# A squared-ReLU MLP by seven products: eight output pairs run their first two products ahead, with results kept in DRAM

## The chip, the cores and the metric

The kernel runs on one core of a Trainium2 chip. Its engines are TensorE (PE; weight loads are shown as PEld), VectorE (DVE), ScalarE (ACT), GpSimd (POOL) and SyncE (SP), whose queue issues nearly all DMA transfers. The metric is the device time of one execution in microseconds; lower is better.

## The reference, cut to what matters

One inference step of a decoder layer: attention and a state-space mixer side by side, then an MLP. The changed code is all in the MLP, over T = 1032 tokens (1024 of a prompt and 8 decoded ones):

```python
x = x + mixed @ w_out                       # (1032, 1024)
u = rms_norm(x, norm_mlp) @ w_up            # 1024 -> 4096
x = x + jnp.square(jax.nn.relu(u)) @ w_down # 4096 -> 1024
```

All values are float32.

## The kernel before, in words

Everything is kept transposed: features on the 128 partitions, tokens along the free axis. Each float32 operand is split (`split`, L131 and L132) into a high part, rounded by ACT to `fp32r`, and a low part, the rest, made by DVE; each product is then three matmuls (high x high, high x low, low x high) that add up in PSUM.

The MLP's first matrix product is computed in blocks. Tokens fall into two halves of HT = 516 columns (H0, H1), input features into two halves of 512 (four partition tiles each), output features into 16 pairs of tiles (2m, 2m+1). For each pair m, seven block products instead of eight make the four output blocks, after sums of weight blocks and of x blocks (a scheme of Strassen's kind). Each product is 4 feature tiles x 3 matmuls x 2 column halves of HC = 258, that is 24 matmuls. They are, in the order of the loop (L1493):

- A: `w1[0:4]` by the first x block (`b11`), copied by ACT to the tile `p1` (`first_product`), then `w1[4:8]` by the second (`b21`) on top of it (`second_product`); the result, after relu and square (`emit_u`, ACT), is stored to the DRAM tensor `u_d`. These two need only the first token half, which is normed and split into `bpr` early.
- five more products, of the weight sums w2, w3, w4 and the x blocks `xva[VT2]`, `VT3`, `VT1`, `VT4`, `V22`, which need the second token half. DVE adds `p1` and PSUM results (L1522, L1528, L1531, L1536, L1540), and six more stores to `u_d` follow.

In this text a pair that runs all seven in the loop is a whole pair, one that runs five a short pair, and the two products run ahead of the loop are an early pair.

Where the second half begins (L1458): the norm factors of that half must be made (`half_stats`, `half_bcast`), then for each of four q the blocks in `xrow` are normed (L1370) and combined (L1473 to L1478; L1477 and L1478 run on POOL), and 20 blocks are split into `xvt`. To give PE something to do meanwhile, the first FP = 4 pairs run as early pairs, with `p1` kept in SBUF (`p1s`).

Weights come from DRAM into `wraw` (two buffers of 512 KB). `wslot` hands out split buffers in a rotation of six: the first two are the `wh`/`wl` buffers of the pool `wp`, the next four are pairs of the pool `opl`, which has eight pairs and whose first eight hold `xrow` (four) and `bpr` (four). `w_first` takes its weights from `wslot`. A whole pair takes four slots, a short pair three.

Preparation of a pair (L1494 to L1510): two raw loads `ra` and `rw`, the additions s1 (L1501), s2, and two in place, and the splits of w2, w3, w4.

The second matrix product (L1569) runs over e, eighths of 512 features of u: load the squares from `u_d` (L1575) through a small tile, split them into four pairs of the pool `up` (6 buffers), which is opened after the pools of the first product are closed, then for each of eight output tiles n three column blocks (384, 384, 264) of 12 matmuls, added by DVE to accumulators `dacc` (L1591).

Within an engine, instructions run in a fixed order that the framework's scheduler has set when the program was built; it need not be the order of the source. A tile that takes over a buffer waits for the last reader of the tile before it.

Of the kernel before, what the change touches and what calls it, by code (L numbers as in the profile page):

```python
# [8 lines left out]
F32 = mybir.dt.float32  # L9
# [45 lines left out]
def hybrid_step(ctx: ExitStack, tc: tile.TileContext, I, O):  # L55
# [3 lines left out]
    def pool(name, bufs=1, **kw):  # L59
        return tc.tile_pool(name=name, bufs=bufs, reuse_waits="tile", **kw)  # L60
# [1312 lines left out]
    NM = 16  # L1373
    FP = 4
    p1s = {}
    slots = [0]
# [81 lines left out]

    xv = mst.enter_context(pool("xv", 1, side="right"))
    VT2, VT3, VT1, VT4, V22 = range(5)  # L1460
    xvt = [[tuple(xv.tile([P, HT], F32R, name=f"x{v}{q}{t}") for t in "hl") for q in range(4)] for v in range(5)]
    xva = [chunk_of(xvt[v], 0) for v in range(5)]
    wa = {0: w_first(0), 1: w_first(1)}
    A = first_product(0, wa[0])
    sv = half_stats(1)
# [3 lines left out]
    for q in range(4):  # L1469
        x11, x12, x21, x22 = xrow[q][:, H0], xrow[q][:, H1], xrow[q + 4][:, H0], xrow[q + 4][:, H1]  # L1470
        normed(q, H1, rb1)
        normed(q + 4, H1, rb1)
        V.tensor_tensor(x11, x12, x11, ALU.subtract)  # L1473
        t2 = mp.tile([P, HT], F32, tag="sa", name="t2")
        V.tensor_tensor(t2, x22, x11, ALU.subtract)
        split(*[t[:] for t in xvt[VT2][q]], t2)
        G.tensor_tensor(x12, x22, x12, ALU.subtract)  # L1477
        G.tensor_tensor(x21, x21, t2, ALU.subtract)  # L1478
        if q:
            if q > 1:  # L1480
                wa[q] = w_first(q)
            A = first_product(q, wa[q])
            second_product(q, wa[q], A)
    for q in range(4):
        split(*[t[:] for t in xvt[VT3][q]], xrow[q][:, H1])
    for q in range(4):
        split(*[t[:] for t in xvt[VT1][q]], xrow[q][:, H0])
    for q in range(4):
        split(*[t[:] for t in xvt[VT4][q]], xrow[q + 4][:, H0])
    for q in range(4):  # L1490
        split(*[t[:] for t in xvt[V22][q]], xrow[q + 4][:, H1])

    for m in range(NM):  # L1493
# [25 lines left out]
        for s in range(2):  # L1519
            prod(X[s], w2, 0, xva[VT2](s), True)  # L1520
            u2.append(mp.tile([P, HC], F32, tag="u2", name="u2"))
            V.tensor_tensor(u2[s], X[s], pc[s], ALU.add)  # L1522
        if m >= FP:
            second_product(m, w1, A)
        for s in range(2):
            prod(X[s], w2, 4, xva[VT3](s), False)
            u3.append(mp.tile([P, HC], F32, tag="u3", name="u3"))
            V.tensor_tensor(u3[s], X[s], pc[s], ALU.add)  # L1528
        for s in range(2):
            prod(Y[s], w3, 0, xva[VT1](s), True)  # L1530
            V.tensor_tensor(u3[s], u3[s], Y[s], ALU.add)  # L1531
            emit_u(2 * m + 1, HT + s * HC, u3[s])
        for s in range(2):
            prod(X[s], w3, 4, xva[VT4](s), False)
            c21 = mp.tile([P, HC], F32, tag="ca", name="c21")
            V.tensor_tensor(c21, X[s], pc[s], ALU.add)  # L1536
            emit_u(2 * m + 1, s * HC, c21)
        for s in range(2):
            prod(Y[s], w4, 0, xva[V22](s), False)
            V.tensor_tensor(u2[s], u2[s], Y[s], ALU.add)  # L1540
            emit_u(2 * m, HT + s * HC, u2[s])
# [27 lines left out]
    for e in range(NE):  # L1569
        ups = [pair(up) for _ in range(FE)]  # L1570
        for c0, cn in CH:
            cs = slice(c0, c0 + cn)
            for f in range(FE):
                r = yp.tile([P, 384], F32, tag="ld", name="ld", bufs=4)
                DQ.dma_start(r[:, :cn], u_d[e * FE + f, :, cs])  # L1575
                split(ups[f][0][:, cs], ups[f][1][:, cs], r[:, :cn])
        uh = lambda k: ups[k][0]
        ul = lambda k: ups[k][1]
        for n2 in range(4):
# [59 lines left out]
```

## Time and profile before

| | |
|---|---|
| runs | 2250.95, 2255.86, 2258.33 us; median 2255.86 |
| the profiled execution | 2256.27 us, span 2254.5 us |
| granted TensorE clock, mean | 0.981 of 2.4 GHz |
| PE busy | 2162.6 us, 96% |
| DVE, ACT, POOL busy | 1365.1, 1013.6, 348.0 us |
| DMA moved | 252.32 MB, mean 112 GB/s |

Times in the profile are microseconds from the start of the span. Matmuls are pipelined, so one shown as 0.28 us follows the one before after 0.12 us; for the length of a piece of work the starts are compared. A part "idle before" in brackets is the time that an engine waited, and what released it. Some matmul records can be missing.

### The profile page before, as it was taken

To read this page: it belongs to the slowest core of one execution; us is meant where nothing else is said; L and a number is where in the kernel's file an instruction comes from. 1 tells how busy PE (TensorE), PEld (TensorE's weight loads), DVE (VectorE), ACT (ScalarE), POOL (GpSimd) and SP (SyncE) were. 2 spreads that over 40 slices of the span, in tenths; PEclk is the share of its full clock that TensorE was granted. 3 is DMA by queue.
4 is the path that set the end of the run, shared out by engine and by line. 5 is a ranking of instruction groups with operands and counts; after the bars stand their busy time and mean duration, and the time that the engine had idled before them with its cause. 6 is when DMAs were issued, how large, how long until landed. Compare 5 with 4: busy or idle time off the path is not lost. (4 is left out here: it accounts for less than half of the span.)

```text
span 2254.5 us, 39182 instructions
## 1 busy us (share of the span) xinstructions
PE 2162.6 (96%) x14859; PEld 2057.8 (91%) x14859; DVE 1365.1 (61%) x2893; ACT 1013.6 (45%) x2044; POOL 348.0 (15%) x409
## 2 busy tenths in 40 slices
PE   6999999998999999999999999996999999999998
PEld 5988899897888898877999999995999998999998
DVE  6778787336846666677355867468655544554452
ACT  3255665235647656666343333345555542221122
POOL 3232232001213222223200013222000000000000
PEclk8999999999999999999999999998999999999999
DMA  4232233322324224123475766642333336332222
GB/s 134 80 109 67 82 90 96 89 61 67 95 67 125 54 82 117 48 81 106 132 229 178 239 186 187 176 146 83 105 109 109 111 98 186 98 110 86 81 93 85
DMA packets 348052, 252.32 MB, mean 112 GB/s; under 512 B 34473, under 2 KB 343929, under 8 KB 347823
## 3 DMA queue, kind: packets, MB, share of 16 engines
q1 hardware_dynamic: 346247, 248.54, 37.3%
q8 instruction: 117, 1.92, 0.4%
q10 hardware_dynamic: 1616, 1.28, 0.2%
q14 instruction: 72, 0.59, 0.1%
HBM read 176.04 MB, written 71.56 MB: 110 GB/s over the span
## 5 line engine op out<-in xcount | busy, mean ns | idle before, releaser
L148 PE MATMUL mm<-hT_h,wh 128*128 128x384 f32 (+1 forms) x1536 | 502.2, 327 | 0.4 <-ACT spill L231 0.4
L149 PE MATMUL mm<-hT_l,wh 128*128 128x384 f32 (+1 forms) x1536 | 493.1, 321 | 0.0
L150 PE MATMUL mm<-hT_h,wl 128*128 128x384 f32 (+1 forms) x1536 | 492.6, 321 | 0.0
L148 PEld LDWEIGHTS mm<-hT_h,wh 128*128 128x128 f32 x1536 | 290.8, 189 | 13.4 <-issue 12.2
L149 PEld LDWEIGHTS mm<-hT_l,wh 128*128 128x128 f32 x1536 | 290.6, 189 | 0.0
L150 PEld LDWEIGHTS mm<-hT_h,wl 128*128 128x128 f32 x1536 | 290.4, 189 | 0.0
L131 ACT ACTIVATE wh<-wraw 128x1024 fp32r<-128x1024 f32 (+1 forms) x158 | 159.9, 1013 | 276.1 <-PE dn L149 153.4
L148 PE MATMUL mm<-oh,wh 128*128 128x384 f32 (+2 forms) x832 | 256.8, 309 | 1.0 <-ACT pr L1289 1.0
L150 PE MATMUL mm<-oh,wl 128*128 128x384 f32 (+2 forms) x832 | 256.3, 308 | 1.4 <-DVE wl L132 1.4
L132 DVE TENSOR_TENSOR wl<-wraw,wh 128x1024 fp32r<-128x1024 f32 (+1 forms) x158 | 185.9, 1177 | 117.1 <-ACT wh L131 111.7
L149 PE MATMUL mm<-ol,wh 128*128 128x384 f32 (+2 forms) x832 | 256.4, 308 | 0.0
L148 PE MATMUL dn<-oh,wh 128*128 128x384 f32 (+1 forms) x768 | 246.4, 323 | 4.2 <-ACT oh L131 4.2
L149 PE MATMUL dn<-ol,wh 128*128 128x384 f32 (+1 forms) x768 | 248.5, 324 | 1.0 <-DVE ol L132 1.0
L150 PE MATMUL dn<-oh,wl 128*128 128x384 f32 (+1 forms) x768 | 246.8, 321 | 0.0
L1591 DVE TENSOR_TENSOR dacc<-dacc,dn 128x384 f32<-128x384 f32 x168 | 85.9, 511 | 151.7 <-PE dn L150 151.7
L148 PEld LDWEIGHTS mm<-oh,wh 128*128 128x128 f32 x832 | 156.6, 188 | 1.7 <-ACT pr L1289 1.5
L150 PEld LDWEIGHTS mm<-oh,wl 128*128 128x128 f32 x832 | 156.6, 188 | 1.6 <-DVE wl L132 1.6
L149 PEld LDWEIGHTS mm<-ol,wh 128*128 128x128 f32 x832 | 156.5, 188 | 0.0
L148 PEld LDWEIGHTS dn<-oh,wh 128*128 128x128 f32 x768 | 145.1, 190 | 5.1 <-ACT oh L131 4.9
L149 PEld LDWEIGHTS dn<-ol,wh 128*128 128x128 f32 x768 | 145.7, 190 | 3.6 <-DVE ol L132 3.4
L150 PEld LDWEIGHTS dn<-oh,wl 128*128 128x128 f32 x768 | 145.5, 189 | 0.0
L131 ACT ACTIVATE oh<-ld 128x384 fp32r<-128x384 f32 (+1 forms) x105 | 48.4, 487 | 122.3 <-PE dn L150 65.1
(952 smaller groups left out, 4573.6 us busy)
## 6 DMA issues: line engine op xcount, KB each, us to landing
wraw<-in_w_in SPq DMA_DIRECT2D x64, 512.0 KB
wraw<-in_w_up SPq DMA_DIRECT2D x36, 512.0 KB
u_d<-u SPq DMA_DIRECT2D x128, 129.0 KB
wraw<-in_w_down SPq DMA_DIRECT2D x32, 512.0 KB
ld<-u_d SPq DMA_DIRECT2D x64, 192.0 KB
xt<-in_x_prompt SPq DMA_DIRECT2D x16, 512.0 KB
s<-in_state_ssm SPq DMA_DIRECT2D x32, 256.0 KB
out_ssm_sample<-s SPq DMA_DIRECT2D x32, 256.0 KB
```

The lines of the kernel that those rows point to most:

```text
L131: first = S.activation(h, src, AF.Copy)
L132: second[:] = [V.tensor_tensor(l, src, h.bitcast(F32), ALU.subtract)]
L148: TE.matmul(ps, lhsT=a, rhs=h, start=k == 0, stop=False)
L149: TE.matmul(ps, lhsT=a, rhs=l, start=False, stop=False)
L150: TE.matmul(ps, lhsT=b, rhs=h, start=False, stop=k == kt - 1)
L1591: V.tensor_tensor(ac[:, cs], prev, ps[:, :cn], ALU.add)
```

## The change

FP goes from 4 to 8: eight early pairs. Their `p1` is stored to a new DRAM tensor `p1_d` and loaded again when the pair's short part runs. Early weights are taken from the two `wh`/`wl` buffers only, not from `wslot`, each traced one early pair ahead; the early pairs are spread over the norming loop and the splits that follow it. The two subtractions that ran on POOL run on DVE. The x blocks live in tiles of T columns (`x23`, `x14`) and `x22`, in a pool that stays open to the end, and these tiles then take the split squares of the second product: `load_ups(0)` is traced in the last pair, `load_ups(e + 1)` ahead of the products of eighth e. The pool `up` is gone, and the accumulators move to the left side of SBUF.

```diff
+    p1_d = dr.tile([8, P, T // 2], F32, name="p1_d")
-    FP = 4
-    p1s = {}
+    FP = 8
     def first_product(m, w):
         p1 = p1t("p1")
-        p1s[m] = p1
         A = [bank(s) for s in range(2)]
         for s in range(2):
             prod(A[s], w, 0, b11(s), True)
             S.activation(p1[:, s * HC:(s + 1) * HC], A[s], AF.Copy)
-        return A
+        if m < FP:
+            DQ.dma_start(p1_d[m], p1)
+        return A, p1
     def w_first(m):
         raw = raw_up(2 * m * P)
-        w = wslot()
+        w = tuple(wp.tile([P, KT, P], F32R, tag=t, name=t) for t in ("wh", "wl"))
         split(w[0], w[1], raw)
         return w
+    def xpair(i):
+        return tuple(xv.tile([P, T], F32R, tag=f"x{i}{t}", name=f"x{i}{t}") for t in "hl")
+    x23 = [xpair(q) for q in range(4)]
+    x14 = [xpair(4 + q) for q in range(4)]
+    def early(m):
+        second_product(m, wa[m], first_product(m, wa[m])[0])
     for q in range(4):
...
-        G.tensor_tensor(x12, x22, x12, ALU.subtract)
-        G.tensor_tensor(x21, x21, t2, ALU.subtract)
-        if q:
-            if q > 1:
-                wa[q] = w_first(q)
-            A = first_product(q, wa[q])
-            second_product(q, wa[q], A)
+        V.tensor_tensor(b12_, b22_, b12_, ALU.subtract)
+        V.tensor_tensor(b21_, b21_, t2, ALU.subtract)
+        early(q + 1)
+        wa[q + 2] = w_first(q + 2)
     for q in range(4):
-        split(*[t[:] for t in xvt[VT3][q]], xrow[q][:, H1])
+        split(x23[q][0][:, H1], x23[q][1][:, H1], xrow[q][:, H1])
+    early(5)
+    wa[6] = w_first(6)
...
+    early(6)
+    wa[7] = w_first(7)
...
+    early(7)
...
+    def load_ups(e, home, step):
+        ups[e] = [xpair(4 * (e % 2) + f) for f in range(4)]
+        for c0 in range(0, T, step):
+            cn = min(step, T - c0)
+            cs = slice(c0, c0 + cn)
+            for f in range(4):
+                r = home()
+                DQ.dma_start(r[:, :cn], u_d[e * 4 + f, :, cs])
+                split(ups[e][f][0][:, cs], ups[e][f][1][:, cs], r[:, :cn])
     for m in range(NM):
...
         if m >= FP:
-            A = first_product(m, w1)
-        p1 = p1s.pop(m)
+            A, p1 = first_product(m, w1)
+        else:
+            p1 = p1t("p1")
+            DQ.dma_start(p1, p1_d[m])
...
+        if m == NM - 1:
+            load_ups(0, lambda: p1t("ld"), HT)
...
-    up = ctx.enter_context(pool("up", 6, side="right"))
-    dap_ = ctx.enter_context(pool("dap", 1, side="right"))
+    dap_ = ctx.enter_context(pool("dap", 1))
...
     for e in range(NE):
-        ups = [pair(up) for _ in range(FE)]
...
+        if e + 1 < NE:
+            load_ups(e + 1, lambda: yp.tile([P, 384], F32, tag="ld", name="ld", bufs=4), 384)
```

In the last pair `load_ups(0)` stands between the products of `x23`'s second half and the three that remain.

## Rows read from the trace of the kernel before

**Rows 1.** The page, part 1: busy time, share of the span, instructions.

```profile
PE 2162.6 (96%) x14859; PEld 2057.8 (91%) x14859; DVE 1365.1 (61%) x2893; ACT 1013.6 (45%) x2044; POOL 348.0 (15%) x409
```

**Rows 2.** PE's waits, 1500 to 2254: waiting line and releaser, total, times, longest.

```profile
PE mm L1398 <- ACT oh L131: 21.0, 1, 21.0
PE dn L148 <- ACT oh L131: 4.2, 1, 4.2
PE dn L1398 <- DVE u L1522: 4.0, 1, 4.0
```

**Rows 3.** Timeline of PE: start, duration, engine, line, operation, out<-in, shape, idle before.

```profile
1523.09 0.28 PE L1400 MATMUL dn<-oh,wl 128*128 128x258 f32 x1
1544.40 0.58 PE L1398 MATMUL mm<-oh 128*128 128x258 f32 x1 [21.03 <-ACT oh L131]
...
1557.88 0.28 PE L1398 MATMUL mm<-x00h,oh 128*128 128x258 f32 x1
...
1572.31 0.28 PE L1398 MATMUL mm<-x00h,wh 128*128 128x258 f32 x1
...
1593.16 0.28 PE L1398 MATMUL mm<-x00h,oh 128*128 128x258 f32 x1
...
1622.81 0.28 PE L1398 MATMUL mm<-oh 128*128 128x258 f32 x1
...
1861.91 0.28 PE L1398 MATMUL mm<-x40h,oh 128*128 128x258 f32 x1
...
1869.14 0.69 PE L148 MATMUL dn<-oh,wh 128*128 128x384 f32 x1 [4.17 <-ACT oh L131]
...
1886.29 0.34 PE L148 MATMUL dn<-oh,wh 128*128 128x384 f32 x1
...
1908.98 0.34 PE L148 MATMUL dn<-oh,wh 128*128 128x384 f32 x1
```

**Rows 4.** Windows of 10 us: PE, PEld, DVE, ACT, POOL busy; granted clock, DMA share, GB/s.

```profile
1540.00:1550.00 10.00, 5.57 (x31) 5.27 (x32) 10.00 (x15) 3.52 (x5) 0.28 (x1) 0.59 0.23 62
1550.00:1560.00 10.00, 10.00 (x86) 10.00 (x85) 8.23 (x14) 6.39 (x15) 0.00 (x0) 1.00 0.34 94
...
1580.00:1590.00 10.00, 9.21 (x58) 9.21 (x59) 7.08 (x14) 4.88 (x11) 0.00 (x0) 0.72 0.24 68
...
1920.00:1930.00 10.00, 9.74 (x56) 8.75 (x56) 7.12 (x15) 4.72 (x10) 0.00 (x0) 1.00 0.63 187
1930.00:1940.00 10.00, 10.00 (x66) 10.00 (x65) 5.27 (x10) 2.00 (x3) 0.00 (x0) 1.00 0.42 131
```

**Rows 5.** Timeline of DVE, 1519 to 1547, columns as in rows 3.

```profile
1519.00 1.42 DVE L1370 SCALAR_TENSOR_TENSOR oh<-oh,prm,rb 128x516 f32<-128x516 f32 x2 [0.97 <-ACT rb L1367]
...
1522.22 1.79 DVE L1370 SCALAR_TENSOR_TENSOR ol<-ol,prm,rb 128x516 f32<-128x516 f32 x1
...
1539.07 1.76 DVE L132 TENSOR_TENSOR x11l<-ol,x11h 128x516 fp32r<-128x516 f32 x1
...
1544.39 1.21 DVE L132 TENSOR_TENSOR ol<-wraw,oh 128x1024 fp32r<-128x1024 f32 x1
1545.53 0.68 DVE L132 TENSOR_TENSOR x23l<-ol,x23h 128x516 fp32r<-128x516 f32 x1
1546.13 0.68 DVE L132 TENSOR_TENSOR x30l<-oh,x30h 128x516 fp32r<-128x516 f32 x1
```

**Rows 6.** Timeline of SP's queue: issues of DMA, columns as in rows 3.

```profile
1505.55 0.38 SPq L1389 DMA_DIRECT2D wraw<-in_w_up  x1
1506.66 3.20 SPq L1342 DMA_DIRECT2D x_d<-ol  x2
...
1572.66 0.38 SPq L1389 DMA_DIRECT2D wraw<-in_w_up  x1
```

**Rows 7.** Timeline of DVE, 1574 to 1581, columns as in rows 3.

```profile
1578.98 0.69 DVE L1501 TENSOR_TENSOR s<-wraw 128x512 f32<-128x512 f32 x1 [4.52 <-DMA wraw<-in_w_up]
...
1580.32 0.42 DVE L1522 TENSOR_TENSOR u<-dn,p 128x258 f32<-128x258 f32 x1
```

**Rows 8.** The chain of work that ended last, at the up product's end.

```profile
1865.34 3.15 DMA ld<-u_d
```

More of the change, by code (lines that the diff above doesn't have):

```diff
@@ L1456, in hybrid_step @@
     rst.close()
[L1459 to L1462, printed above, removed]
+    xv = ctx.enter_context(pool("xv", 1, side="right"))
+    def xpair(i):
+        return tuple(xv.tile([P, T], F32R, tag=f"x{i}{t}", name=f"x{i}{t}") for t in "hl")
+    x23 = [xpair(q) for q in range(4)]
+    x14 = [xpair(4 + q) for q in range(4)]
+    x22 = [tuple(xv.tile([P, HT], F32R, name=f"v{q}{t}") for t in "hl") for q in range(4)]
+    vt2, vt3, vt1, vt4, v22 = chunk_of(x23, 0), chunk_of(x23, HT), chunk_of(x14, 0), chunk_of(x14, HT), chunk_of(x22, 0)
     wa = {0: w_first(0), 1: w_first(1)}
-    A = first_product(0, wa[0])
+    def early(m):
+        second_product(m, wa[m], first_product(m, wa[m])[0])
+    A = first_product(0, wa[0])[0]
     sv = half_stats(1)
@@ L1469, in hybrid_step @@
     for q in range(4):
-        x11, x12, x21, x22 = xrow[q][:, H0], xrow[q][:, H1], xrow[q + 4][:, H0], xrow[q + 4][:, H1]
+        b11_, b12_, b21_, b22_ = xrow[q][:, H0], xrow[q][:, H1], xrow[q + 4][:, H0], xrow[q + 4][:, H1]
         normed(q, H1, rb1)
         normed(q + 4, H1, rb1)
-        V.tensor_tensor(x11, x12, x11, ALU.subtract)
+        V.tensor_tensor(b11_, b12_, b11_, ALU.subtract)
         t2 = mp.tile([P, HT], F32, tag="sa", name="t2")
-        V.tensor_tensor(t2, x22, x11, ALU.subtract)
-        split(*[t[:] for t in xvt[VT2][q]], t2)
-        G.tensor_tensor(x12, x22, x12, ALU.subtract)
-        G.tensor_tensor(x21, x21, t2, ALU.subtract)
-        if q:
-            if q > 1:
-                wa[q] = w_first(q)
-            A = first_product(q, wa[q])
-            second_product(q, wa[q], A)
+        V.tensor_tensor(t2, b22_, b11_, ALU.subtract)
+        split(x23[q][0][:, H0], x23[q][1][:, H0], t2)
+        V.tensor_tensor(b12_, b22_, b12_, ALU.subtract)
+        V.tensor_tensor(b21_, b21_, t2, ALU.subtract)
+        early(q + 1)
+        wa[q + 2] = w_first(q + 2)
     for q in range(4):
-        split(*[t[:] for t in xvt[VT3][q]], xrow[q][:, H1])
+        split(x23[q][0][:, H1], x23[q][1][:, H1], xrow[q][:, H1])
+    early(5)
+    wa[6] = w_first(6)
     for q in range(4):
-        split(*[t[:] for t in xvt[VT1][q]], xrow[q][:, H0])
+        split(x14[q][0][:, H0], x14[q][1][:, H0], xrow[q][:, H0])
+    early(6)
+    wa[7] = w_first(7)
     for q in range(4):
-        split(*[t[:] for t in xvt[VT4][q]], xrow[q + 4][:, H0])
+        split(x14[q][0][:, H1], x14[q][1][:, H1], xrow[q + 4][:, H0])
+    early(7)
     for q in range(4):
-        split(*[t[:] for t in xvt[V22][q]], xrow[q + 4][:, H1])
+        split(x22[q][0][:], x22[q][1][:], xrow[q + 4][:, H1])
+    ups = {}
+    def load_ups(e, home, step):
[7 more added lines that the diff above has]
+                split(ups[e][f][0][:, cs], ups[e][f][1][:, cs], r[:, :cn])
     for m in range(NM):
@@ L1538, in hybrid_step @@
         for s in range(2):
-            prod(Y[s], w4, 0, xva[V22](s), False)
+            prod(Y[s], w4, 0, v22(s), False)
             V.tensor_tensor(u2[s], u2[s], Y[s], ALU.add)
@@ L1569, in hybrid_step @@
     for e in range(NE):
-        ups = [pair(up) for _ in range(FE)]
[L1571 to L1578, printed above, removed]
+        if e + 1 < NE:
+            load_ups(e + 1, lambda: yp.tile([P, 384], F32, tag="ld", name="ld", bufs=4), 384)
+        uh = lambda k: ups[e][k][0]
+        ul = lambda k: ups[e][k][1]
         for n2 in range(4):
```

8 lines of the change are left out of this document (4 added, 4 removed).

## The prediction

> **What bounds the kernel now.** I read the page first: TensorE (PE) is busy for 96% of the span [rows 1]. So no engine is to be made faster; what can be won is the time in which PE waits or runs at the lower clock. PE's waits come next, from 1500 us on, where all the changed code runs. The reader is to see that three waits make nearly all of it: 21.0 us for an ACT split, 4.0 us for a DVE addition, 4.2 us at the start of the down product [rows 2]. PE's own timeline then gives the times at which one piece of work ends and the next begins [rows 3].
>
> First the unit. Pair 0 runs its five products (each 24 matmuls, both column halves) from 1557.88 to 1572.31, that is 2.88 us a product [rows 3]. An early pair (two products) is 5.76 us, a short pair (five) 14.4, a whole pair (seven) 20.2. Between the end of early pair 1 (last matmul at 1523.09, and 0.12 for its own step) and the start of pair 4 (1622.81) lie 99.6 us. The work there is two early and four short pairs, 11.5 + 57.8 = 69.3 us, so 30.3 us are lost: 21.2 up to 1544.40; 2.0 in early pairs 2 and 3, which take 13.48 instead of 11.5 (granted clock 0.59 there, a mix of 1.2 and 2.4 GHz [rows 4]); nothing in pair 0; 6.4 in pair 1 (20.85), of which 4.0 is the wait and the rest half clock (0.72 [rows 4]); 0.8 in pairs 2 and 3. From pair 4 to 15 nothing is lost: the last product of the up stage starts at 1861.91, so it ends at 1864.79, twelve times 20.17 after 1622.81.
>
> The down product starts 4.35 us later, and its first two blocks of 36 matmuls take 1886.29 - 1869.14 = 17.15 us where the next four (to 1908.98) take 5.67 each [rows 3]: 5.8 more, 10.2 together. At the second eighth of the down product 56 matmuls run in 10 us instead of 66, 1.5 us [rows 4]. All that the change can reach is 30.3 + 10.2 + 1.5 = 42.0 us; the number of matmuls does not change. The profiled execution took 2256.27 us, 1.8 over its span and 0.4 over the median of the three runs (2255.86), so **2214.3 us** is the floor, and the question is what of the 42.0 stays or comes back elsewhere.
>
> **Why the 21 us.** The weights of early pairs 2 and 3 go into `opl` pairs that hold `xrow`, so their split waits until DVE has read those [rows 2]. DVE is busy without a hole meanwhile [rows 4]. In the changed kernel early weights use only the two `wh`/`wl` buffers, free once the early pair two before has run. The dependence on all of DVE's work goes; in its place comes one on the part of it traced ahead of each split.
>
> **The early part, step by step.** A `normed` costs DVE 1.42 / 2 = 0.71; an addition or split of 516 columns 0.60 to 0.61 and a weight split 1.14 from start to start [rows 5]. One q of the loop is now 2 x 0.71 + 5 x 0.61 = 4.5, with its weight split 5.6 us, against 5.76 us of PE. From 1519.0 on, weights 2 are there at 1524.6, 1.4 us after PE has ended early pair 1; from then on DVE gains 0.2 us on each pair. After the loop come 16 splits of x (9.8 us) and two of weights (2.3), beside three early pairs (17.3 us). DVE's sum, 22.4 + 9.8 + 2.3 = 34.5 us, ends at 1553.5; PE ends early pair 7 at 1523.2 + 1.4 + 34.6 = 1559.2. ACT has room: with two early pairs and pair 0's preparation it was busy 6.4 of 10 us [rows 4]. I charge **2 us**; bounds 0 (order better than traced) and 10 (half of the old wait, should x splits stand in front of the weights).
>
> The eight subtractions that leave POOL cost DVE 8 x 0.61 = 4.9 us. But a DVE operation beside a POOL one took 1.76 to 1.79 us instead of 0.68 to 0.71; there are eight such, of which the first and the last are shown [rows 5], so 8 x 1.08 = 8.6 us go. Net 3.7 us less on DVE. The Trainium skill, Perfetto Trace Analysis, section Optimizing Scalar/DVE Operations, says that with DVE saturated it may make sense to move work off it, even to GpSimd, and warns that the two share an SBUF read port. By its first half alone this step would be wrong here, 4.9 us more on DVE; by its warning it is right, and the trace agrees with the warning.
>
> The raw weights: SP takes its instructions in a fixed order, but not the source's. Weights 2 were issued at 1505.55, ahead of a store that is traced before them (1506.66) [rows 6]. A raw buffer is free with the split two early pairs before, so a load has about 9 us until it is needed; one took from 1572.66 [rows 6] to 1578.98 [rows 7], 6.3 us. Hidden.
>
> **p1 through DRAM** adds eight stores and eight loads of 264 KB on SP. The nearest rows are a load of 192 KB, 3.15 us [rows 8], and the 512 KB one, 6.3. Five buffers let a load run several pairs ahead, and a pair lasts 14.4 us, so I take 0; without that cover it is 3 to 6 us per pair, 24 to 50. Nothing else is short of DMA: its share was at most 0.34 in the stretches shown up to 1590 [rows 4].
>
> **Short pairs, eight in place of four.** Each needs two raw loads, nine DVE operations of preparation and three weight buffers in 14.4 us. Before, one of them stalled: a raw load of pair 2 was issued only at 1572.66 [rows 6], after the last split of pair 1 that read its buffer; the addition s1 (L1501) stood at the head of DVE until 1578.98, and behind it L1522, for which PE waited [rows 7]. The following short pairs lost 0.8 together: the loop of load and preparation is shorter than a pair and gets ahead. So it is a cost of starting up, and the start is much the same (raw loads only once the last early weights are split). I take the **7.2 us** of before again (6.4 + 0.8); bounds 0 and twice, 14.4.
>
> **Transition.** The squares of the first eighth are now loaded, and split into x23, while pair 15 has three products left, 8.6 us. The DMA has free buffers well before; DVE's part, eight splits, is 4.9 us. The wait of 4.2 and the half clock after it need not come. New: `wslot` is called 56 times, not 64, so in pair 15 the two `wh` buffers hold w3 and w4 instead of w1 and w2, and the first down weights can be split only 2.9 us before the end, among the last additions. I charge **2.5 us**, bounds 0 and 10.2 (all as before). The 1.5 us at the second eighth go, as those squares have their own buffers now.
>
> Sum: 2256.3 - 42.0 + 2 + 0 + 7.2 + 2.5 = **2226 us**.
>
> **Rivals.**
> 1. *Clean*: nothing stays, 2214. For it: pairs 4 to 15 run 242 us without a hole. Against: one bad place in DVE's order is enough for a stall, as in pair 1. 12%.
> 2. *Early pairs bound by their weights.* If SP has the load of weights m+2 behind the stores of early pair m, it is issued 1 us after that pair, lands 6.3 later, and ACT and DVE add 2.2: 9.5 us against 5.76, so 3.7 us in each of five gaps, 19 in place of the 2: 2243. For it: SP's stores wait for ACT, and what is behind them waits too. Against: the load at 1505.55, put ahead. 13%.
> 3. *The transition gains nothing*, the late `wh` buffers and ACT's backlog giving the old 10.2: 2234. 8%.
> 4. *Slower*: s1 stands ahead of L1522 in DVE's order in every short pair, and its raw load is late in every one. Price 6.4 us, eight times 51: 2214.3 + 2 + 51 + 2.5 = 2270. It decides from six stalls on (42.0 - 4.5 = 37.5 us to lose). For it: more DMA per short pair than before, by a p1 load. Against: of the four such pairs before only one paid. 5%.
> 5. *The order does not use the freedom* (early weights split only after all of x, as before): within 0.3% of 2256. 4%.
>
> The forecast, 2216 to 2236, keeps 58%. **The range** takes in the bounds of the unknown costs: low 2213, high 2214.3 + 10 + 14.4 + 10.2 = 2249; rivals 4 and 5, 9%, stay out. 0.3%, some 7 us, is about what a measurement of this kernel can tell from no change. Faster 0.89, same 0.06, slower 0.05.
>
> **What would show it.** Right: in PE's waits the 21 us row is gone or under 3; the granted clock is 1.00 from 1520 on but for one short pair; pair 0 begins near 1560 with eight early pairs done; the up stage ends near 1844 and the down product starts within 3 us of it; POOL has nothing after 1512. Wrong: PE waits for a weight split in each early pair (rival 2); PE waits for L1522's successor in many short pairs while DVE waits for raw loads (rival 4); or for an addition whose p1 has just landed, which would make the 0 for DRAM wrong.

## The result and the profile after

The changed kernel takes **2232.96 us** (median of four runs, 2226.27 to 2236.17) where the kernel before took 2255.89 beside it: a ratio of **0.9897, 95% interval 0.9869 to 0.9926**. Timed again next to the experiments it took 2232.68, a ratio of 0.9892 (0.9879 to 0.9906). So it is about 1.05% faster; 1.3% was forecast. The profiled execution took 2236.17 us, its span is 2234.5.

First the page, part 1 (busy time, share of the span, instructions), as in [rows 1]: PE is busy 6.3 us less in a span that is 20 us shorter, and POOL has lost the eight subtractions.

```profile
PE 2156.3 (97%) x14859; PEld 2053.8 (92%) x14859; DVE 1359.0 (61%) x2897; ACT 1006.5 (45%) x2040; POOL 334.2 (15%) x401
```

Next PE's waits from 1500 to 2240, the same view as [rows 2] (waiting line and releaser, total, times, longest). Lines of the changed kernel are numbered anew: L1522 of before is L1549 here, s1 (L1501) is L1526, the split of helper L131 is L132.

```profile
PE mm L1398 <- DVE u L1549: 5.9, 3, 3.0
PE dn L149 <- ACT wh L132: 3.6, 1, 3.6
PE mm L1398 <- ACT p L1426: 1.2, 1, 1.2
PE mm L1398 <- ACT u L1414: 1.1, 2, 0.6
PE dn L1398 <- DVE u L1549: 1.0, 1, 1.0
```

The 21.0 us row is gone. What is left is small: 8.0 us of waits in the short pairs and 3.6 us at the start of the down product. PE's timeline (columns as in [rows 3]) places them. The first row is the sum of squares of the second half, at which the code common to both kernels ends; then come the one wait of the early part, the start of pair 0, two of the stalls in the short pairs, the last matmul of the up product and the first of the down product.

```profile
1516.54 0.62 PE L1355 MATMUL pstat<-ones,acc 128*86 128x1 f32 x7
...
1560.82 0.38 PE L1398 MATMUL mm<-oh,wh 128*128 128x258 f32 x1 [1.21 <-ACT p L1426]
...
1563.80 0.28 PE L1398 MATMUL mm<-x0h,wh 128*128 128x258 f32 x1
...
1583.69 0.39 PE L1398 MATMUL dn<-x0h,oh 128*128 128x258 f32 x1 [1.03 <-DVE u L1549]
...
1599.96 0.58 PE L1398 MATMUL mm<-x0h,wh 128*128 128x258 f32 x1 [3.04 <-DVE u L1549]
...
1850.70 0.28 PE L1400 MATMUL dn<-v3h,wl 128*128 128x258 f32 x1
...
1854.63 0.44 PE L149 MATMUL dn<-x0h,wh 128*128 128x384 f32 x1 [3.64 <-ACT wh L132]
```

From the start of these statistics to pair 0 it takes 47.3 us, with eight early pairs behind it; before, 46.1 with four (pair 0 at 1557.88 in [rows 3]). In the kernel before the statistics start here:

```profile
1511.74 0.47 PE L1354 MATMUL pstat<-ones,acc 128*86 128x1 f32 x5
```

Windows (columns as in [rows 4]) show the early part full, and the two places between 1520 and 2200 where the granted clock still falls below 1.00, in the third short pair and at the start of the down product:

```profile
1530.00:1540.00 10.00, 10.00 (x86) 10.00 (x85) 10.00 (x15) 9.75 (x22) 0.00 (x0) 1.00 0.52 153
1595.00:1605.00 10.00, 6.96 (x46) 6.75 (x46) 5.91 (x12) 3.85 (x8) 0.00 (x0) 0.83 0.37 123
1850.00:1860.00 10.00, 6.30 (x30) 5.88 (x29) 7.78 (x14) 7.40 (x17) 0.00 (x0) 0.83 0.86 257
```

**One table for all kernels.** PE's timeline gives four times in each profile: the start of those statistics (S), the first matmul of pair 0 (P), the end of the up product (U, last matmul and 0.12) and the end of the span (E). The loss ahead of pair 0 is P - S less 45.9 us for eight early pairs (22.8 for four, 4 x 5.76 less); 45.9 is what e2 took, where PE waits for nothing there. The loss in the up product is U - P less 14.4 for each short pair and 20.16 for each whole one. All in us; medians are from several chips, and each ratio is to the kernel before on the same chip.

| kernel | median | ratio, 95% | S | P - S | loss | U - P | loss | E - U | E - S |
|---|---|---|---|---|---|---|---|---|---|
| before | 2255.9 | 1 | 1511.7 | 46.1 | 23.3 | 306.9 | 7.4 | 389.7 | 742.8 |
| changed | 2233.0 | 0.9897 (0.9869 to 0.9926) | 1516.5 | 47.3 | 1.4 | 287.0 | 10.5 | 383.7 | 718.0 |
| e5: changed, again | 2232.7 | 0.9892 (0.9879 to 0.9906) | 1517.0 | 47.1 | 1.2 | 285.5 | 9.0 | 383.5 | 716.1 |
| e1: second squares later | 2225.8 | 0.9876 (0.9858 to 0.9894) | 1512.1 | 47.2 | 1.3 | 285.9 | 9.4 | 379.6 | 712.7 |
| e2: four raw buffers | 2221.7 | 0.9857 (0.9839 to 0.9874) | 1512.3 | 45.9 | 0 | 276.6 | 0.1 | 384.1 | 706.6 |
| e3: e1 and e2 | 2223.1 | 0.9860 (0.9842 to 0.9878) | 1513.7 | 45.9 | 0 | 278.3 | 1.8 | 383.8 | 707.9 |
| e8: e3, other homes | 2219.3 | 0.9831 (0.9818 to 0.9845) | 1514.5 | 45.9 | 0 | 277.9 | 1.4 | 379.0 | 702.7 |
| e4: before, own buffers | 2254.7 | 0.9999 (0.9988 to 1.0010) | 1511.2 | 41.8 | 19.0 | 309.0 | 9.5 | 389.0 | 739.8 |
| e6: changed, xrow buffers | 2251.1 | 0.9972 (0.9962 to 0.9982) | 1514.0 | 69.3 | 23.4 | 284.0 | 7.5 | 384.2 | 737.5 |
| e12: changed, four early | 2246.2 | 0.9943 (0.9926 to 0.9959) | 1514.7 | 38.1 | 15.2 | 308.5 | 8.9 | 383.0 | 729.5 |
| e7: changed, POOL | 2241.0 | 0.9924 (0.9912 to 0.9937) | 1510.8 | 55.7 | 9.8 | 284.4 | 7.9 | 383.4 | 723.5 |
| e9: p1 traffic twice | 2232.6 | 0.9894 (0.9879 to 0.9909) | 1513.1 | 49.8 | 4.0 | 284.1 | 7.7 | 383.6 | 717.6 |
| e10: first squares late | 2231.2 | 0.9885 (0.9869 to 0.9902) | 1514.1 | 47.2 | 1.3 | 284.7 | 8.2 | 384.3 | 716.1 |
| e11: before, p1 scratch | 2255.4 | 0.9993 (0.9983 to 1.0003) | 1509.8 | 46.1 | 23.3 | 305.1 | 5.5 | 388.5 | 739.6 |

S itself varies from 1509.8 to 1517.0, so kernels are best compared by E - S, and by medians where these settle it. E - S too varies: 742.8 and 739.6 for before and e11, 718.0 and 716.1 for the changed kernel twice. A difference of 2 to 3 us between two single profiles decides nothing.

### The profile page after: what moved, and what is told of

Read it like the earlier page. It is cut to its first block, busy times and chain, and to the rows that moved or that the text cites. A ratio compares the mean times of both kernels' runs of the same rounds, so it can differ in the third digit from the quotient of the medians.

```text
span 2234.5 us, 39207 instructions
## 1 busy us (share of the span) xinstructions
PE 2156.3 (97%) x14859; PEld 2053.8 (92%) x14859; DVE 1359.0 (61%) x2897; ACT 1006.5 (45%) x2040; POOL 334.2 (15%) x401
## 4 chain that ended last, share of the span: by engine, by line
PE 71%; DMA 8%; DVE 6%; ACT 3%; issue 2%; SPq 0%; POOL 0%; ACTq 0%; DVEq 0%; POOLq 0%
PE mm L149 12%; PE mm L150 12%; PE mm L151 12%; PE dn L151 5%; PE dn L149 5%; PE dn L150 5%; PE mm L1398 2%; PE mm L1399 2%; PE mm L1400 2%; PE dn L1398 2%; PE dn L1399 2%; PE dn L1400 2%; DMA wraw<-in_w_up 2%; PE psy L1116 1%; DMA ld<-yz_d 1%
## 5 line engine op out<-in xcount | busy, mean ns | idle before, releaser
L132 ACT ACTIVATE wh<-wraw 128x1024 fp32r<-128x1024 f32 (+1 forms) x164 | 165.6, 1012 | 303.2 <-PE dn L150 181.6
L133 DVE TENSOR_TENSOR wl<-wraw,wh 128x1024 fp32r<-128x1024 f32 (+1 forms) x164 | 192.5, 1175 | 115.2 <-ACT wh L132 113.6
L616 DVE SCALAR_TENSOR_TENSOR xc<-raw,prm,xc 128x1024 f32<-128x1024 f32 x72 | 93.6, 1300 | 7.0 <-ACT xc L613 6.9
L768 ACT ACTIVATE cm<-cm,nm,rq 128x128 f32<-128x128 f32 x128 | 61.7, 483 | 54.8 <-DVE nm L764 54.8
L1031 DVE SCALAR_TENSOR_TENSOR s<-s,dap,uu 128x128 f32<-128x128 f32 x128 | 48.9, 409 | 36.3 <-ACT uu L1030 36.1
L1306 POOL TENSOR_TENSOR gr<-gr,rs 128x384 f32<-128x384 f32 (+1 forms) x24 | 28.0, 1167 | 275.5 <-ACT gr L1305 261.9
L1030 ACT ACTIVATE uu<-bcb,dtp 128x128 f32<-128x128 f32 x128 | 42.4, 391 | 54.5 <-DMA bcb<-bc_d 53.4
L1268 DVE STREAM_TRANSPOSE xo<-xt 32x256 f32<-32x256 f32 x128 | 55.8, 436 | 9.5 <-DMA xT_d<-xo 5.3
L608 ACT ACTIVATE raw<-mm 128x384 f32<-128x384 f32 (+1 forms) x72 | 32.1, 447 | 60.2 <-PE mm L151 60.2
```

The source lines that it names most:

```text
L132: first = S.activation(h, src, AF.Copy)
L133: second[:] = [V.tensor_tensor(l, src, h.bitcast(F32), ALU.subtract)]
L616: V.scalar_tensor_tensor(out[:, :NP], raw[:, k:k + NP], wk, out[:, :NP], ALU.mult, ALU.add)
L768: S.activation(cm[:, h, :], cm[:, h, :], AF.Exp, bias=nm[:, h:h + 1], scale=rq[:, j, h:h + 1], accum_out=sm[:, h:h + 1])
L1268: V.transpose(xo[32 * j:32 * j + 32, :, 32 * i:32 * i + 32], xb[32 * i:32 * i + 32, :, j, :])
```

## What the 21 us were: the runs on the early part

The forecast put the 21 us down to one dependence: weights 2 and 3 went into buffers of `xrow`, which DVE had still to read. The change does two things about it, own buffers for early weights and eight early pairs instead of four. Two runs (e4 and e6) make a square of it with the kernel before and the changed one. It is not quite clean: the changed kernel and e6 also have the subtractions on DVE and p1 in DRAM, which the other two have not.

**e4: before, with own weight buffers.**

```diff
     def w_first(m):
         raw = raw_up(2 * m * P)
-        w = wslot()
+        w = tuple(wp.tile([P, KT, P], F32R, tag=t, name=t) for t in ("wh", "wl"))
```

> The kernel before with one part of the change: its four early pairs take their weights into the two wh and wl buffers, never into the buffers of xrow. Nothing else is changed, POOL's subtractions and p1 in SBUF included. Theory: the 21 us wait is the dependence on xrow's buffers, so it goes from early pair 2; but with only two early pairs left as cover (11.5 us), PE has done them near 1537 and then waits for the preparation of pair 0, which stands behind DVE's splits of x until some 1553. So 5 to 12 us are won of the 21, 2244 to 2251, and the wait moves to the start of pair 0. Rival A: the dependence was all, pair 0 is ready at once and 2235 comes out: then eight early pairs are not needed. Rival B: nothing is won (2256), DVE's work alone sets the start of pair 0 and the dependence cost nothing.

It brought nothing: 0.9999. The single wait of 21.0 us is now two. PE's waits from 1500 to 1560 in this kernel:

```profile
PE mm L1400 <- DVE wl L132: 8.1, 1, 8.1
PE mm L1398 <- ACT wh L131: 6.6, 1, 6.6
```

The first is early pair 3 waiting for its weights, the second pair 0 waiting for its own (until 1552.99). Pair 0 starts 4.3 us sooner after S (41.8 instead of 46.1), and the 2 us that the up product then loses more are within what two profiles of one kernel differ by. By E - S it gains 3.0 on the profile of before and nothing on that of e11, which up to the MLP is the same. So the theory was right in kind (a wait moves to pair 0) and too high in its gain of 5 to 12; rival B, that nothing is won because DVE's work alone sets pair 0, has it nearly right.

**e6: the changed kernel, its early weights through the buffers of `xrow`.**

```diff
     def w_first(m):
         raw = raw_up(2 * m * P)
-        w = tuple(wp.tile([P, KT, P], F32R, tag=t, name=t) for t in ("wh", "wl"))
+        w = wslot()
```

> The changed kernel with one part undone: eight early pairs, but early weights 2 to 5 go through the buffers of xrow again, as in the kernel before. With the run before (four early pairs, own buffers: no gain) this makes a square of two by two. Theory of the forecast (the dependence on xrow costs the 21 us): early pair 2 waits some 20 to 25 us until DVE has read xrow, six early pairs still stand behind that wait, and the time is 2250 to 2256. Rival (only the missing cover cost, the number of early pairs): the wait stays under 5 us and the time near 2233.

2251.1, as the theory said (2250 to 2256): of the gain a quarter is left. The wait itself is shorter than its 20 to 25; these are the longest of PE's waits from 1500 to 1600:

```profile
PE mm L1398 <- ACT oh L132: 17.4, 1, 17.4
PE mm L1398 <- ACT p L1426: 2.0, 2, 1.3
```

With eight pairs the dependence costs 69.3 - 47.2 = 22 us ahead of pair 0; with four it cost 4.3 (before against e4). Neither half of the change does anything much alone: the loss ahead of pair 0 is 23.3 with neither, 19.0 with own buffers, 23.4 with eight pairs, 1.4 with both.

**e12: the changed kernel with four early pairs.**

```diff
-    FP = 8
+    FP = 4
...
-        early(q + 1)
-        wa[q + 2] = w_first(q + 2)
+        if q < 3:
+            early(q + 1)
+        if q < 2:
+            wa[q + 2] = w_first(q + 2)
...
-    early(5)
-    wa[6] = w_first(6)
...
-    early(6)
-    wa[7] = w_first(7)
...
-    early(7)
```

> The changed kernel with one part undone: four early pairs, not eight (own weight buffers, DVE alone, p1 through DRAM and the early first squares stay). Theory from the runs so far: up to pair 0 DVE has some 33 to 38 us of work after the statistics, and four early pairs with the statistics are 22.8 us of work for the PE, so 10 to 15 us are lost ahead of pair 0, where eight pairs (45.9 us) lost 1; the short pairs lose about 7 as with four of them before, the rest is as in the changed kernel, 383.5 from the up product's end; from the statistics to the end some 725 us, the median 2239 to 2244. Rival: without POOL and without the wait on xrow DVE keeps ahead of four pairs too; then pair 0 starts some 24 us after the statistics and the time is 2228 to 2231, and the four further pairs buy nothing.

2246.2, a little above the theory's 2239 to 2244; 15.2 us lost ahead of pair 0, where 10 to 15 were expected. Windows of that kernel from the end of PE's cover on (columns as in [rows 4]) show what sets it:

```profile
1535.00:1545.00 10.00, 2.51 (x21) 2.31 (x20) 10.00 (x17) 5.95 (x13) 0.00 (x0) 0.86 0.51 157
1545.00:1555.00 10.00, 2.27 (x10) 2.27 (x11) 9.97 (x18) 2.71 (x5) 0.00 (x0) 0.50 0.00 0
```

and PE's timeline the price:

```profile
1537.23 0.28 PE L1400 MATMUL dn<-oh,wl 128*128 128x258 f32 x1
1552.73 0.58 PE L1398 MATMUL mm<-x0h,wh 128*128 128x258 f32 x1 [15.21 <-ACT wh L132]
```

The third column of busy times is DVE: it hardly stops, while PE, in the first, is done at 1537. Now the parts add up. DVE's preparation lets pair 0 start 38.1 us after S (e12). With the subtractions on POOL it is 41.8 (e4), 3.7 more; with the dependence on `xrow` as well 46.1 (before), 4.3 more. PE's cover is 22.8 us with four early pairs and 45.9 with eight. With eight, DVE has four more weight splits at 1.14 [rows 5], so an estimate is 38.1 + 4.6 = 42.7; in the changed kernel's timeline the first weight split of pair 0 ends at 1561.63, 45.1 after S, with 1.3 of waiting for a raw load ahead of it. Either way that is the first time that PE's cover is the longer of the two, by less than 1 us in the trace: eight pairs are just enough. **In the kernel before, two things held pair 0 back one behind the other: the dependence on `xrow`, and behind it DVE's work, for which four early pairs are too little cover. Own buffers alone (e4) or more cover alone (e6) win at most 4.3 us ahead of pair 0; only both together win 22.**

**e7: the subtractions back on POOL.**

```diff
-        V.tensor_tensor(b12_, b22_, b12_, ALU.subtract)
-        V.tensor_tensor(b21_, b21_, t2, ALU.subtract)
+        G.tensor_tensor(b12_, b22_, b12_, ALU.subtract)
+        G.tensor_tensor(b21_, b21_, t2, ALU.subtract)
```

> The changed kernel with the eight subtractions back on POOL. Theory: eight DVE operations beside them take 1.76 us again, not 0.68, so DVE is 8.6 - 4.9 = 3.7 us later with x and with pair 0; the PE has about 1 us in hand at pair 0, and the time is 2 to 4 us more than the unedited kernel beside it, with PE waiting for DVE or ACT between 1545 and 1570. Rival: a saturated DVE gains by what is taken off it, 4.9 us; then PE waits no more than before, and the time is the same or 1 us less.

2241.0, 8.3 us more than e5 beside it, and P - S is 8.5 more than there (55.7 and 47.1, both rounded): twice the 2 to 4 expected. The DVE rows do nearly what the forecast says, with seven such long operations for its eight (timeline of DVE, columns as in [rows 3]): of two neighbours the one ahead takes 0.68, and the next, beside a POOL subtraction that runs from 1525.23 to 1526.90, takes 1.77.

```profile
1525.07 0.68 DVE L133 TENSOR_TENSOR x0l<-t,x0h 128x516 fp32r<-128x516 f32 x1
1525.68 1.77 DVE L1485 TENSOR_TENSOR t<-ol 128x516 f32<-128x516 f32 x1
```

What the forecast's sum of DVE's time leaves out stands in the timelines of POOL, ACT and PE; this is the longest place:

```profile
1532.30 3.46 POOL L1487 TENSOR_TENSOR oh<-oh 128x516 f32<-128x516 f32 x1 [2.57 <-DVE oh L1483]
...
1535.80 0.63 ACT L132 ACTIVATE x2h<-oh 128x516 fp32r<-128x516 f32 x1 [3.51 <-POOL oh L1487]
...
1537.17 0.36 ACT L1426 ACTIVATE p<-mm 128x258 f32<-128x258 f32 x1
...
1537.59 0.58 PE L1398 MATMUL mm<-oh,wh 128*128 128x258 f32 x1 [3.93 <-ACT p L1426]
```

POOL's subtraction takes 3.46 us, ACT stands 3.51 us before the split of its result, the copy `p` that empties PE's bank stands behind that split on ACT, and PE waits 3.93 for the bank. Two shorter waits for `p` (1.26 and 1.04) and a granted clock of 0.86 from 1530 to 1540, where the changed kernel has 1.00, come on top. The Trainium skill, Perfetto Trace Analysis, section Optimizing Scalar/DVE Operations, says that moving work off a saturated DVE, even to GpSimd, may make sense, and warns of the SBUF read port that the two share; this run agrees with the warning (1.77 against 0.68), and here the move cost 8.3 us.

**e9: the traffic of p1 doubled.**

```diff
             DQ.dma_start(p1_d[m], p1)
+            DQ.dma_start(p1_d[m], p1)
...
             DQ.dma_start(p1, p1_d[m])
+            DQ.dma_start(p1, p1_d[m])
```

> The changed kernel with every store of p1 to DRAM and every load of it issued twice: 8 more stores and 8 more loads of 264 KB, and as many more instructions in SP's queue. Theory of the forecast (the detour of p1 costs nothing, its cover is a whole pair): the stretch from the statistics to the end stays at 716 to 718 us, no wait of the PE for a sum that waits for p1, and the median within 2 us of 2232.7. Rival: the DMA engines (0.86 busy between 1560 and 1570 us) or SP's queue are full there; then raw loads land later, the short pairs lose 3 to 10 us more, and the detour has a price of about that size in the changed kernel too.

2232.6 against 2232.7: no price in the whole, though not none in every part. Ahead of pair 0 it loses 2.7 us more, in one wait for the copy `p` (PE's waits from 1500 to 1700), and the short pairs lose less (7.7 instead of 9.0 to 10.5).

```profile
PE dn L1398 <- ACT p L1426: 2.7, 1, 2.7
```

So in the whole the detour through DRAM is hidden, as the forecast took it. Where the waits for `p` come from, the traces tell. These are rows of the changed kernel, DVE's first and then ACT's:

```profile
1558.42 0.69 DVE L1526 TENSOR_TENSOR s<-wraw 128x512 f32<-128x512 f32 x1 [1.31 <-DMA wraw<-in_w_up]
1559.87 0.63 ACT L132 ACTIVATE wh<-s 128x512 fp32r<-128x512 f32 x1 [2.26 <-DVE s L1527]
1560.40 0.37 ACT L1426 ACTIVATE p<-mm 128x258 f32<-128x258 f32 x1
```

The second raw load of pair 0 was issued at 1553.49, when the last early weights had been read out of its buffer (1553.46); DVE waits for it, ACT for DVE's second addition, and the copy `p` stands behind on ACT. So the 1.2 us belong to the raw buffers and not to the stores of p1, and in e2, with four raw buffers, they are gone. In e9 the same chain is longer: its buffer had been read at 1550.04, but the load was issued only at 1552.75, and DVE waits 3.67 us for it. There the edit does have a price at one place, as the rival said of SP's queue, but the whole doesn't show it.

## The short pairs

**e2: four buffers for raw weights in place of two.** The place comes from `p1`, which gets two buffers; `rb1` and the first squares go through raw buffers.

```diff
-    p1t = lambda name: mp.tile([P, HT], F32, tag="p1", name=name, bufs=5)
+    p1t = lambda name: mp.tile([P, HT], F32, tag="p1", name=name, bufs=2)
...
+    def raw_tile(own):
+        if own:
+            return mp.tile([P, KT * P], F32, tag="rw", name="rw", bufs=2)
+        return wp.tile([P, KT, P], F32, tag="wraw", name="wraw")[:].rearrange("p k n -> p (k n)")
...
-    rb1 = p1t("rb1")
+    rb1 = raw_tile(True)[:, 0:HT]
...
-            load_ups(0, lambda: p1t("ld"), HT)
+            ld = (raw_tile(i % 2 == 0) for i in range(8))
+            load_ups(0, lambda: next(ld), HT)
...
-        ra, rw = raw_up(2 * m * P), raw_up((2 * m + 1) * P)
+        ra, rw = raw_up(2 * m * P), raw_up((2 * m + 1) * P, True)
```

> Two more buffers of 4 KB for the raw weights of the up product (those of the second load of a pair); the place comes from p1, which has 2 buffers, not 5, and rb1 and the first squares go through raw buffers. Theory: short pairs lose 10.6 us because a raw load of pair m+1 is issued only with the last split of pair m, lands when the pair has begun, and the addition s1 holds the head of DVE's queue for it (3.7 us at 1598.15). With four buffers DVE's waits for the raw load in the short pairs go from 10 us to under 2, the eight short pairs lose about 3 us, and the time is about 2226. Rival: the stalls come from the order of DVE and the buffers of the sums (2.9 us for ACT u at 1583.21), and the time stays within 2 us of 2233. If p1 through DRAM lives by its five buffers, PE waits for sums that wait for p1, and the kernel is slower, some 3 us for each pair.

2221.7, better than the theory's 2226; by the ratios (0.9857, and 0.9892 for e5) the gain is 7.9 us, near the 7 of the theory. The loss in the up product goes from 9.0 or 10.5 to 0.1. In the changed kernel the chain is the one that the forecast read in the kernel before [rows 6, 7], on SP and DVE:

```profile
1592.14 0.38 SPq L1389 DMA_DIRECT2D wraw<-in_w_up  x1
...
1598.15 0.69 DVE L1526 TENSOR_TENSOR s<-wraw 128x512 f32<-128x512 f32 x1 [3.66 <-DMA wraw<-in_w_up]
1598.87 0.69 DVE L1527 TENSOR_TENSOR s<-s,wraw 128x512 f32<-128x512 f32 x1
1599.48 0.42 DVE L1549 TENSOR_TENSOR u<-mm,p 128x258 f32<-128x258 f32 x1
```

A raw load issued at 1592.14 lands at 1598.15; s1 has the head of DVE until then; L1549 runs behind it, and PE goes on at 1599.96. In the later pairs s1 is less late, but the whole preparation is, so that its last split stands just ahead of the next pair's L1549 (PE waits 1.59 until 1647.17):

```profile
1637.17 0.69 DVE L1526 TENSOR_TENSOR s<-wraw 128x512 f32<-128x512 f32 x1 [2.64 <-DMA wraw<-in_w_up]
...
1645.99 0.69 DVE L133 TENSOR_TENSOR ol<-wraw,oh 128x512 fp32r<-128x512 f32 x1 [0.56 <-ACT oh L132]
1646.60 0.42 DVE L1549 TENSOR_TENSOR u<-mm,p 128x258 f32<-128x258 f32 x1
```

Not every stall is of this kind: the one of 1.03 us until 1583.69 comes from an L1549 that waited 2.92 us for ACT, which had waited 3.81 for a store to `u_d`, and two of 0.5 us are waits for ACT. In e2 all of them are gone; through which of its edits, no run tells. DVE's waits for raw loads from 1560 to 1690, first in the changed kernel, then the longest of e2:

```profile
DVE s L1526 <- DMA wraw<-in_w_up: 14.8, 9, 3.7
```

```profile
DVE rw L1535 <- DMA wraw<-in_w_up: 1.0, 1, 1.0
```

The run also shows that two buffers of `p1` do as well as five: PE waits for nothing between S and the end of the up product. That the raw loads did it, and not what had to make room for them, is argued only: fewer `p1` buffers take freedom away, and the other two moves lie ahead of pair 0 and behind the short pairs.

## The start of the down product

**e1: the squares of the second eighth later.**

```diff
     for e in range(NE):
-        if e + 1 < NE:
-            load_ups(e + 1, lambda: yp.tile([P, 384], F32, tag="ld", name="ld", bufs=4), 384)
...
         for n2 in range(4):
             wh, wl = load_w(w_dn, n2 * 256, k0=e * FE, kt=FE, ncol=256)
...
+            if n2 == 0 and e + 1 < NE:
+                load_ups(e + 1, lambda: yp.tile([P, 384], F32, tag="ld", name="ld", bufs=4), 384)
```

> The loads and splits of the second eighth's squares are traced after the first weight group of the first eighth, not ahead of it. Theory: in the changed kernel the down product starts 3.6 us late (and runs at half clock until about 1859) because ACT takes the splits x4h to x7h of the second eighth, and their waits for u_d, ahead of the first wh. Then the wait for ACT wh falls from 3.6 us to under 1, the 6.1 us of the transition to about 1.5, and the median from 2233 to about 2228. Rival: the wh buffers, free only with the products of pair 15, or the raw weights hold the split; then the 3.6 us stay, and the time stays within 1 us of 2233. Either way the second eighth must still start without a hole; if its squares come too late, PE waits there instead and the gain is lost.

The theory came from ACT's timeline in the changed kernel. The four splits x4h to x7h are of the second eighth, not needed until the first eighth's products are done (about 1902), and they and the waits between them stand ahead of the first `wh` of the down product:

```profile
1850.53 0.51 ACT L132 ACTIVATE x5h<-ld 128x384 fp32r<-128x384 f32 x1
...
1851.59 0.52 ACT L132 ACTIVATE x6h<-ld 128x384 fp32r<-128x384 f32 x1 [0.23 <-DMA ld<-u_d]
1852.49 0.42 ACT L1413 ACTIVATE u<-u 128x258 f32<-128x258 f32 x1 [0.38 <-DMA u_d<-u]
1852.82 0.51 ACT L132 ACTIVATE x7h<-ld 128x384 fp32r<-128x384 f32 x1
...
1853.54 1.04 ACT L132 ACTIVATE wh<-wraw 128x1024 fp32r<-128x1024 f32 x1
```

In e1 PE's waits from 1800 to 1900 are these:

```profile
PE dn L151 <- DVE wl L133: 0.6, 1, 0.6
PE dn L149 <- DVE dacc L1612: 0.5, 1, 0.5
PE dn L149 <- ACT wh L132: 0.2, 1, 0.2
```

The wait for `wh` falls from 3.6 to 0.2, and from the up product's end to the end of the span it takes 379.6 us instead of 383.7 and 383.5, a gain of 4. So the place of these squares was the cause; the edit moves their loads as well as their splits, but in the rows above ACT comes to that `wh` without a gap, so neither its raw weights nor its buffers hold it, only ACT's own queue. The median of 2225.8 is another 3 us lower than that explains; its comparison is with 2253.7 for the kernel before on that chip, and by the ratios (0.9876, and 0.9892 for e5) the gain is 1.6 per mille, 3.6 us.

**e10: the squares of the first eighth late again.**

```diff
-        if m == NM - 1:
-            load_ups(0, lambda: p1t("ld"), HT)
...
+    ld = lambda: yp.tile([P, 384], F32, tag="ld", name="ld", bufs=4)
     for e in range(NE):
+        if e == 0:
+            load_ups(0, ld, 384)
```

> The changed kernel with one part undone: the squares of the first eighth are not loaded in the last pair but at the start of the down product, ahead of those of the second eighth, in the same buffers as these. Theory: the early load gains 4 us of the 10.2 that the kernel before lost there (6.1 are left in the changed kernel), so the transition loses some 10 to 12 us again and the median is 2237 to 2239. Rival: ACT's queue (splits of the second eighth ahead of the first wh) sets the start either way, and the median stays at 2233. With the run of the later second squares (1 to 1.5 us lost) this sets the early load and the order on ACT apart.

2231.2: the rival's answer, and the early load gains nothing that can be measured while the second eighth's squares stand where they do (E - U is 384.3, against 383.5 and 383.7). The loss is only in another place. PE's waits from 1800 to 1900 in this kernel:

```profile
PE dn L149 <- DVE dacc L1615: 4.1, 2, 3.1
PE dn L149 <- ACT x0h L132: 0.6, 1, 0.6
PE dn L149 <- ACT x2h L132: 0.3, 1, 0.3
```

The first `wh` is in time here, but the splits of the second eighth still stand ahead of the sums `dacc` on DVE, and PE waits for those, some 18 us into the down product. So with the second eighth's squares traced first, it doesn't matter when the first eighth's are loaded. A late load of the first squares together with e1's order was not tried. The other 5.4 us between before (389.7) and this run belong to what it still shares with the changed kernel, buffers of their own for the squares among it; which part of that, no run tells.

**e3 and e8: both edits.** e3 is e1 and e2 in one kernel.

> The two edits of the runs before together. They touch stages 160 us apart, so the gains should add: about 2221 if both theories hold (5 from the transition, 7 from the short pairs), 2228 or 2226 if one does, 2233 if none.

2223.1 instead of 2221: the short pairs gain as in e2 (1.8 lost), but the wait for `wh` is back with 3.3 us. ACT's timeline tells why:

```profile
1840.17 1.06 ACT L132 ACTIVATE wh<-wraw 128x1024 fp32r<-128x1024 f32 x1 [1.97 <-DMA wraw<-in_w_down]
```

The first squares had gone through the raw buffers that the first down weights need. e8 gives them others:

```diff
-            ld = (raw_tile(i % 2 == 0) for i in range(8))
+            ld = (raw_tile(True) if i % 2 == 0 else mp.tile([P, HT], F32, tag="sa", name="ld") for i in range(8))
```

> The two edits again (later second squares, four raw buffers), with the first squares loaded through the second raw buffers and those of s1 and s2, not through the buffers of the raw weights that the first down weights need too. Theory: the 3.3 us that PE waited for the first wh in the run of both came from those buffers (ACT waited 2.0 us for the raw down weights); so the wait goes, from the statistics to the end it takes 702 us, not 707.9, and the time is 2217. Rival: the first down weights come late for another reason, and the wait and the 2223 stay.

E - S is 702.7 (702 expected) and the median 2219.3 (2217 expected), a ratio of **0.9831 (0.9818 to 0.9845)** to the kernel before and 13.3 us under e5 beside it: the best kernel of these. All of PE's waits from 1500 to 2215 in it:

```profile
PE mm L1403 <- DVE u L1554: 1.1, 1, 1.1
PE psy L1592 <- ACT yo L1595: 1.0, 1, 1.0
PE dn L151 <- DVE wl L133: 0.6, 1, 0.6
```

## Ahead of the MLP

In the changed kernel S came 4.8 us later than in the kernel before, although no instruction ahead of it is changed. Two runs ask whether the change has a part in that.

> The changed kernel once more, unedited, as the base for the small steps beside it. In its first profile the code ahead of the MLP, which the change doesn't touch, ended 4.8 us later than in the kernel before (the statistics of the second half at 1516.54, against 1511.74), while in the four runs profiled since they were at 1511.20 to 1513.71. Theory: this is a difference from run to run; so the statistics fall near 1512 to 1514 this time, the stretch from there to the end takes 718 us again (742.8 before), and the median is 2228 to 2232. Rival: the change itself delays the code ahead of it by its order of instructions; then they are near 1516 again, and the median is 2233.

> The kernel before with nothing but the scratch tensor of p1 in DRAM (2.1 MB, placed among the others) and one store of p1 in early pair 3. All engines run the same instructions up to the MLP in the kernel before and in the changed one, yet the statistics stood at 1511.2 and 1511.7 in the two profiles without that tensor and at 1510.8 to 1517.0, 1513.9 in the mean, in the eight with it. Theory: run to run; the statistics fall anywhere in that range, and the median is that of the kernel before within 0.1%. Rival: the scratch moves the addresses of the other tensors in DRAM, and transfers ahead of the MLP take 2 to 3 us longer: a ratio of 1.001 or more, whose interval leaves out 1.

e5 is the changed kernel unedited; e11 has this:

```diff
+    p1_d = dr.tile([8, P, T // 2], F32, name="p1_d")
...
             S.activation(p1[:, s * HC:(s + 1) * HC], A[s], AF.Copy)
+        if m == 3:
+            DQ.dma_start(p1_d[m], p1)
```

In e5 S is 1517.0, so the theory missed there, and the median 2232.7; in e11 S is 1509.8, the earliest of all, and the ratio 0.9993 (0.9983 to 1.0003): the place of the scratch in DRAM costs nothing. e7, in which the order of instructions ahead of S is that of the changed kernel, had S at 1510.8. I take it for a variation of executions, not an effect of the change, but two profiles of the changed kernel that both came late leave that open.

## Why the forecast was right, and where it was off

2226 was forecast, 2233 came: inside the range, 7.0 above the sum. By its steps:

**The floor and what is lost.** The loss of the kernel before and its places were read rightly: e8, which takes away what is left in the short pairs and at the down product's start, comes within 2 us of the floor after S (702.7; the forecast's floor is 742.8 - 42.0 = 700.8).

**Why the 21 us: right in its sum, half of it in its reason.** The step named the dependence on `xrow` alone. e6 leaves that in and loses most of the gain, so it is one half; but e4 took it away alone and won nothing. The next paragraph had the other half in numbers, without drawing it: it set DVE's end beside PE's for eight pairs, but not for four, where 22.8 us of PE stand against 38.1 of DVE (e12). The change does both things, and so the sum came out.

**The early part: 2 charged, 1.4 and 1.2 measured.** Pair 0 begins 47.3 us after S, at 1563.80 (near 1560 was forecast; S itself came 4.8 later than before). The granted clock is 1.00 throughout. That the size fits is in part luck. The forecast's 1.4 us for late weights 2 did not come: DVE split them ahead of the norms, by 1523.02, and PE did not wait. What came instead is the copy `p` behind the preparation of pair 0 (the chain shown with e9), and that preparation, with its raw load, stands in no sum of the forecast: DVE's sum ended at 1553.5, 41.8 after S, and pair 0's first weights were split at 45.1.

**POOL to DVE: net 3.7 less on DVE, and 3.7 between e12 and e4** (38.1 and 41.8). These two differ in more than the subtractions, but from 8 us after S on DVE has no hole up to pair 0 in either. Its price in the changed kernel is 8.3 (e7), since ACT, which splits POOL's results in order, passes POOL's delay on to PE. POOL's last row in the changed kernel is at 1515.21, just ahead of S.

**p1 through DRAM: 0, right in the whole** (e9). With two buffers instead of five it still holds (e2).

**Short pairs: 7.2 charged, 9.0 and 10.5 measured.** The mechanism was right, s1 at the head of DVE waiting for a raw load, with the addition that PE needs behind it; e2 takes away the loads' lateness and the loss goes. The size was off: the forecast took it for a cost of starting up, paid by one pair. Here six of eight pairs pay, 0.5 to 3.0 us each. Load and preparation (raw loads issued at 1576 to 1579, 1590 to 1592) take nearly the 14.4 us of a pair and gain on it only slowly; that this alone is the reason is argued, since e2 changes more than the raw buffers, and one stall began with a store. The longest is s1 ahead of the addition itself; in the later ones it is the preparation that is late behind s1. That is rival 4's mechanism with a fifth of its price.

**Transition: 2.5 charged over 378.0, 5.7 and 5.5 measured.** This is the worst of the terms. The forecast feared the last additions and the late `wh` buffers; it counted ACT's own queue only as a rival (3, with all of 10.2). What stood there were the splits of the second eighth, which the change traces ahead of the first down weights; the forecast spoke of those squares only as a gain of 1.5 us. The 4 us are theirs (e1). That the early load of the first squares would bring the gain is not borne out: without it the time is the same (e10).

**The rest.** The three terms are 11.7 in the forecast and 15.7 to 17.6 in the two profiles, so 4 to 6 of the 7.0. The remaining 1 to 3 lie ahead of S or in the difference of single runs.

Of the rivals, 1 (clean, 2214) was not reached by the changed kernel but nearly by e8 (2219); 2 did not come, no early pair but the last waits at all; of 3 half came, through ACT's queue; 4 came in small; 5 did not come.

## What to carry to other kernels

A wait on one name says which dependence came last, not what removing it is worth: before crediting a change with the whole of it, add up the work of the releasing engine up to that point and compare it with the work that the waiting engine can do meanwhile. Where load and preparation of a step take nearly as long as the step, look at the buffers of the load: with four raw buffers, and what made room for them, the loss of the up product went from 9 to 10.5 us down to 0.1 here. And what is traced early for a later stage takes its place in an in-order queue ahead of what the next stage needs first.

## What the runs showed of the hardware

A POOL subtraction of 128x516 took 1.67 to 3.46 us in e7, and one DVE operation beside it 1.77 instead of 0.68; such a pair of durations had been read from the kernel before [rows 5]. New is how far it reaches: through the splits that ACT takes in order, ACT stood still for 3.51 us and PE for 3.93.

The stretch ahead of the MLP, in which all fourteen profiles run the same work, ended between 1509.8 and 1517.0 us. The spread of 7 us is as large as the error of the forecast; it is why single profiles were compared from S on.
